# Shift of the first modulation by dot products on VectorE, its late columns behind the first emptying of PSUM, and the late modulation columns on GpSimd and ScalarE during attention

## The chip, the cores and the metric

The kernel runs on one core of one Trainium2 chip. The metric is the device time of one execution in microseconds (us). Five engines work from queues of their own, each in order: TensorE (PE, with its weight loads PEld), VectorE (DVE), ScalarE (ACT), GpSimd (POOL) and SyncE (SP), which issues most DMAs. Matrix products land in PSUM, everything else lies in SBUF.

## The reference: what is computed

One layer of an encoder with two head groups, over 1024 tokens of width 1024, all float32:

```python
mod = silu(c) @ w_ada + b_ada                 # 6 x 1024 columns
sh1, sc1, g1, sh2, sc2, g2 = split(mod, 6)
h = rms_norm(x, g) * (1 + sc1) + sh1
proj = h @ w_in                               # q, k, v | conv q/k, v, o, gates
y = concat(attention(q, k, v), bidirectional_mlstm(...))
x = x + g1 * (y @ w_out)
h = rms_norm(x, g') * (1 + sc2) + sh2
x = x + g2 * ((silu(h @ w_gate) * (h @ w_up)) @ w_down)
return rms_norm(x, g'')
```

Attention has 8 query heads on 2 key heads, with a norm and a rotary turn on q and k. The mLSTM has 4 heads, run forward and backward in chunks, behind a convolution over 5 tokens. The 48 groups of 128 modulation columns are 48 dot products of `silu(c)` with rows of the transposed `w_ada`.

## The kernel before: stages, queues and names

The kernel is written with an explicit order. A small event clock inside it (`Clock`, `Engine`, `Stream`) estimates the engines while the program is built, and the instructions are emitted in the order in which that clock reaches them. So an edit at one place moves instructions at others, far behind it. Nothing is moved when the program runs: each engine executes its list as written, and waits where an operand isn't there. Every matrix product of two float32 operands is done as three products of rounded parts (`mm3`, lines 307 to 310): `whi*x_hi`, `whi*x_lo`, `wlo*x_hi`; `whi` is made by ACT, `wlo` by POOL or DVE.

The stages, with their place in the profiled execution:

- **Opening, 0 to about 198 us.** The first three products (k, v and the first q pair; tiles `acc`, 6 PSUM banks) are computed from `x * sc1` without the root of the norm and without the shift. The norm's root is applied when PSUM is emptied (`vt`, `raw_q`: the DVE rows `vt<-acc` and `raw_q<-acc`), and the shift's part, a number per output column, is added later: `shift_sums` (line 621) multiplies the three weight blocks, loaded a second time as `wagain`, with the shift column `sh2` in 24 small matmuls (line 629). Its result `shift` releases `shifted` in `v_steps` and `rope_steps`. The other products need the complete `h` (tiles `hh`, `hl`, made by `h_steps`, line 664: DVE multiply, ACT affine with shift column `mod[:, k]`, ACT rounding, POOL remainder). `chunk_step` fills `acct` tiles from `h`, which take the PSUM banks of the first products as these come free. After that come the gates of the mLSTM (`gate_steps`: scans on DVE, transposes `T` on PE, results `cols` and `dec`) and the first units of `IN`, until `rope_ok[3]` and `gates_ok` are there.
- **Attention, about 198 to 512 us.** Three streams, `scores` (tile `S`, softmax on DVE, ACT, POOL: `sst`, `P`), `turned` (transposes `T` into `PT`) and `values` (`av`), 64 blocks. Where none of them can go on, PE is given units of `IN`, the remaining input projections: `f` (convolution, tile `acc`, `xp`, `y`) and `t` (tile `acct`).
- **mLSTM, 512 to about 690 us.** Streams of states (`U`, `Cs`), fronts (`E`, `W`) and backs (`na`, `ni`, `num`); the rest of `IN` and then the output projection (`o`) fill the gaps.
- **FFN, to the end.** It fills PE almost wholly.

The modulation columns: 16 large tiles `ada` (128x1024) in the opening give scale and shift; columns 4 to 7 of the shift wait for the flag `late` besides, which is set with the norm's root (line 707). The other 32 groups come as 64 half tiles (128x512) through `ada_late` (line 1069): at most two in flight, each one DMA on SP and one DVE multiply with `accum_out`. It is called from the opening's loops, from `ready()`, once in each of the 64 blocks of `scores`, and with each step of the streams in the mLSTM. 48 of them must be done at the end of attention; the last 16 follow in the mLSTM, and when `IN` has run out there, a loop (`while not summed`) emits what is left of the 16 before anything else.

Of the kernel before, what the change touches and what calls it, by code (L numbers as in the profile page):

```python
# [247 lines left out]
def layer_kernel(ctx, tc, xT, c, w_ada, vecs, cons, rope, w_f, w_t0, w_t, w_o, w_gu, w_d, out):  # L248
# [112 lines left out]
    with tc.manual_schedule():  # L361
# [161 lines left out]
        sh2 = stp.tile([P, KT, 2], F32, name="sh2")  # L523
# [97 lines left out]
        def shift_sums():  # L621

            ck.need(slot("acc").flag())
            acc, f = psum_tile([P, 3, 2], "acc")
            for f3 in range(3):
                ck.need(again[f3])
                w = wagain[f3].rearrange("p (a b) -> p a b", a=KT)
                for k in range(KT):
                    nc.tensor.matmul(acc[:, f3], w[:, k], sh2[:, k], start=k == 0, stop=k == KT - 1)
# [10 lines left out]
            ck.chain(LAT, take, gains, flag=shift_ok)  # L640
# [37 lines left out]
        for k in range(KT):  # L678
# [15 lines left out]
            if k == 5:  # L694
# [12 lines left out]
                ck.chain(0.0, *rstd_ok, lambda: None, flag=late)  # L707
# [1560 lines left out]
```

## Time and profile before

| | |
|---|---|
| runs | 1410.9 us median of 3 (1406.38 to 1412.68) |
| profiled execution | 1413.44 us, of it span 1411.7 us |
| PE busy | 1291.5 us (91%), mean granted clock 0.958 |
| DVE, ACT, POOL busy | 1068.9 us (76%), 673.2 us (48%), 634.4 us (45%) |
| half tiles `ada` on DVE, 52.4 to 197.7 us, 197.7 to 512 us, 512 to 690 us | 36.61 us (with 4 of the large), 16.65 us, 14.23 us |

Rows of a timeline give start, length, engine, line, operation, `out<-in`, shapes, and in brackets how long the engine had stood idle and who released it. L96 is the helper that records every operation of DVE, ACT and POOL, so these are told apart by their tiles. A windows row gives the busy time of each engine in that stretch, then the granted clock of PE, the DMA share and GB/s. A row of grouped instructions gives busy time and mean ns of one.

### The profile page before, as it was taken

Reading aid. Unit: us, or ns where it says so; the run is one execution under the profiler, and the core shown is the slowest. Engines: PE = TensorE matmul, PEld = TensorE weight load, DVE = VectorE, ACT = ScalarE, POOL = GpSimd, SP = SyncE. Lnnn points to the kernel's source line nnn. Section 1 sums busy time; section 2 is a strip of 40 time slices with the busy share of each in tenths; the row PEclk is TensorE's granted clock in tenths of the full one; section 3 lists DMA queues with packets and bytes.
Section 4 is the critical chain, followed back from the end, with each engine's and each line's share of the span. In section 5 each row is a group of like instructions: output and inputs, shape, how many; then the busy total and the mean of one; then the engine's idle time right before and its main releaser. Section 6 shows DMA issues by size and latency. Waiting matters only on the chain.

```text
span 1411.7 us, 19611 instructions
## 1 busy us (share of the span) xinstructions
PE 1291.5 (91%) x6632; PEld 1087.6 (77%) x6640; DVE 1068.9 (76%) x1623; ACT 673.2 (48%) x1217; POOL 634.4 (45%) x537
## 2 busy tenths in 40 slices
PE   7799779999999993989799799999999999979997
PEld 5597658898888892877677588888888887857887
DVE  7948989977888634888598897666766654998876
ACT  6654336576666652555377423233323333444462
POOL 0445434344444224667403165455455445545542
PEclk9889879999999996999899899999999999989999
DMA  9554542322122146633454243233222248733324
GB/s 353 179 165 146 161 157 72 113 72 56 54 70 60 51 141 205 226 115 117 140 168 145 70 152 102 105 113 112 103 82 94 96 164 310 303 84 102 98 64 154
DMA packets 103892, 185.98 MB, mean 132 GB/s; under 512 B 11376, under 2 KB 33136, under 8 KB 103792
## 3 DMA queue, kind: packets, MB, share of 16 engines
q1 hardware_dynamic: 90400, 162.63, 36.1%
q10 hardware_dynamic: 13392, 22.10, 4.1%
q8 instruction: 53, 0.87, 0.3%
q14 instruction: 47, 0.39, 0.1%
HBM read 137.76 MB, written 43.25 MB: 128 GB/s over the span
## 4 chain that ended last, share of the span: by engine, by line
PE 63%; DVE 22%; issue 5%; DMA 4%; ACT 3%; POOL 2%; SPq 0%; ACTq 0%; DVEq 0%; POOLq 0%
PE acc L310 16%; PE acc L309 16%; PE acc L308 16%; PE av L1164 3%; DVE sst L96 3%; DVE ada L96 3%; DVE y L96 3%; PE T L1145 2%; PE S L1113 2%; DVE PT L96 2%; DVE x L96 2%; PE acct L308 2%; PE acct L309 1%; PE acct L310 1%; DMA ada<-in_w_ada_dram 1%
## 5 line engine op out<-in xcount | busy, mean ns | idle before, releaser
L96 POOL TENSOR_TENSOR wlo<-wst,whi 128x512 fp32r<-128x512 f32 (+2 forms) x187 | 264.3, 1420 | 297.3 <-ACT whi L96 266.7
L96 ACT ACTIVATE whi<-wst 128x512 fp32r<-128x512 f32 (+2 forms) x219 | 130.9, 605 | 106.2 <-PE acc L310 32.9
L96 POOL TENSOR_SCALAR P<-P,sst 128x1024 f32<-128x1024 f32 x64 | 81.8, 1279 | 163.8 <-DVE sst L96 136.8
L309 PE MATMUL acc<-x,whi 128*128 128x512 f32 x352 | 138.4, 393 | 5.9 <-DVE x L96 5.9
L96 POOL TENSOR_TENSOR wlo<-wr,whi 128x512 fp32r<-128x512 f32 x56 | 77.7, 1388 | 75.2 <-ACT whi L96 70.5
L308 PE MATMUL acc<-whi,wch 128*128 128x512 f32 x244 | 96.5, 396 | 7.0 <-ACT wch L96 7.0
L310 PE MATMUL acc<-whi,wcl 128*128 128x512 f32 x244 | 96.7, 396 | 2.9 <-DVE wcl L96 2.8
L308 PE MATMUL acc<-hh,whi 128*128 128x512 f32 x224 | 96.2, 429 | 2.2 <-ACT xp L96 2.1
L96 DVE SCALAR_TENSOR_TENSOR ada<-ada,cond 128x512 f32<-128x512 f32 (+1 forms) x80 | 81.4, 1029 | 21.4 <-DMA ada<-in_w_ada_dram 13.0
L309 PE MATMUL acc<-wlo,wch 128*128 128x512 f32 x244 | 96.1, 394 | 0.1
L96 DVE TENSOR_TENSOR PT<-T,PT 128x512 fp32r<-128x512 f32 x128 | 83.5, 683 | 13.8 <-ACT PT L96 13.4
L96 ACT ACTIVATE P<-S,sst,colq 128x1024 f32<-128x1024 f32 x64 | 77.2, 1207 | 33.7 <-DVE sst L96 32.5
L96 ACT ACTIVATE PT<-T 128x512 fp32r<-128x512 f32 x128 | 72.1, 596 | 38.1 <-PE T L1145 37.4
L309 PE MATMUL acc<-hl,whi 128*128 128x512 f32 x224 | 90.0, 402 | 0.0
L308 PE MATMUL acct<-whi,hh 128*128 128x256 f32 (+1 forms) x256 | 80.0, 312 | 11.0 <-DVE vt L96 9.9
L310 PE MATMUL acc<-hh,wlo 128*128 128x512 f32 x224 | 89.9, 402 | 0.0
L96 ACT ACTIVATE whi<-wr 128x512 fp32r<-128x512 f32 x60 | 37.9, 632 | 105.1 <-DVE wr L96 50.1
L96 DVE TENSOR_TENSOR sg<-acc,sg 128x512 f32<-128x512 f32 x67 | 45.4, 687 | 55.7 <-PE acc L310 55.5
L96 POOL TENSOR_TENSOR wlo<-s,whi 128x512 fp32r<-128x512 f32 x40 | 53.9, 1349 | 67.2 <-ACT whi L96 67.2
L96 DVE TENSOR_REDUCE sst<-S 128x1 f32<-128x1024 f32 x64 | 77.8, 1216 | 6.8 <-PE S L1113 6.5
L309 PEld LDWEIGHTS acc<-x,whi 128*128 128x128 f32 x352 | 66.7, 189 | 21.0 <-DVE x L96 7.3
L96 DVE TENSOR_TENSOR wcl<-wd,wch 128x512 fp32r<-128x512 f32 x50 | 50.7, 1028 | 37.6 <-ACT wch L96 27.1
(474 smaller groups left out, 3812.1 us busy)
## 6 DMA issues: line engine op xcount, KB each, us to landing
wr<-in_w_gu_dram SPq DMA_DIRECT2D x66, 256.0 KB, 2.7
ada<-in_w_ada_dram SPq DMA_DIRECT2D x64, 256.0 KB, 3.2
wd<-in_w_d_dram SPq DMA_DIRECT2D x22, 512.0 KB, 7.0
wst<-in_w_gu_dram SPq DMA_DIRECT2D x34, 256.0 KB, 3.0
wst<-act_d SPq DMA_DIRECT2D x33, 256.0 KB, 4.8
ada<-in_w_ada_dram SPq DMA_DIRECT2D x16, 512.0 KB, 6.8
wst<-in_w_o_dram SPq DMA_DIRECT2D x32, 256.0 KB, 3.5
act_d<-sg ACTq DMA_DIRECT2D x31, 256.0 KB, 2.2
```

The lines of the kernel that those rows point to most:

```text
L96: return fn(*args, **kw)
L308: nc.tensor.matmul(acc, w[0], x[0], start=first, stop=False)
L309: nc.tensor.matmul(acc, w[0], x[1], start=False, stop=False)
L310: nc.tensor.matmul(acc, w[1], x[0], start=False, stop=last)
L1113: nc.tensor.matmul(sp[:, halves(n)], qs[:, j * P:(j + 1) * P], k2[g][m][:, halves(n)], start=m == 0, stop=m == 1)
L1145: nc.tensor.transpose(tp[:, k], Pt[q][:, (4 * b + k) * P:(4 * b + k + 1) * P], ident)
L1164: nc.tensor.matmul(av, va[:, k, h // 4], PT[it][m][:, k], start=(k, m) == (0, 0), stop=(k, m) == (NJ - 1, 1))
```

## The change

1. **Shift's part.** ACT writes a `diag` tile: 8 blocks of the identity, each scaled by one shift column. PE multiplies it by `ones` in two 128x512 matmuls, which leaves the shift as a row in every partition, in two PSUM banks of the `acc` ring. DVE multiplies it with the transposed weights (`w_fT`, a new input of the same bytes as the three blocks of `w_f`) in six 128x512 operations with `accum_out`, and adds the halves. The 24 small matmuls go.
2. **Late columns.** `late` is now set when the six first PSUM banks are empty, so the four large DVE products of shift columns 4 to 7 stand behind `vt` and `raw_q`. The remainder `hl` of the first tile is made by DVE, not POOL. The PSUM bank of the second half of query 1 is taken after the chunk loop.
3. **Modulation columns.** `ada_late` isn't called in the opening any more. The first 48 half tiles all fall to attention, and there each is a POOL multiply and an ACT copy with `accum_out`. The last 16 stay on DVE in the mLSTM.

```diff
@@ shift_sums
-                for k in range(KT):
-                    nc.tensor.matmul(acc[:, f3], w[:, k], sh2[:, k], start=k == 0, stop=k == KT - 1)
...
+                rows.append(psum_tile([P, HALF], "acc"))
+                nc.tensor.matmul(rows[i][0], ones, diag[0][:, halves(i)], start=True, stop=True)
...
+                dve.scalar_tensor_tensor(w, w, 1.0, rows[i][0], op0=OP.mult, op1=OP.mult, accum_out=sh2[:, f3, i:i + 1])
...
+                dve.tensor_add(shift, sh2[:, :, 0], sh2[:, :, 1])
...
+                act.activation(diag[0][:, k * P:(k + 1) * P], ident, AF.Copy, scale=mod[:, k:k + 1])
@@ load_again
-                again[i] = ck.chain(dma(w, w_f[i].rearrange("p a b -> p (a b)")), lambda: None)
+                again[i] = ck.chain(dma(w, w_fT[i]), lambda: None)
@@ h_steps
-                lambda: gps.tensor_sub(h_lo[k][:, halves(n)], xs, h_hi[k][:, halves(n)].bitcast(F32)))
+                lambda: (gps if n or k else dve).tensor_sub(h_lo[k][:, halves(n)], xs, h_hi[k][:, halves(n)].bitcast(F32)))
@@ the opening's order
-                ck.chain(0.0, *rstd_ok, lambda: None, flag=late)
+        ck.chain(0.0, *[f for a in acc0 for _, f in a], lambda: None, flag=late)
...
-                ada_late()
@@ ada_late
+            if n < 48:
+                adas.append(ck.chain(dma(t, w_ada[j][:, halves(i)]), lambda: gps.tensor_mul(t, t, PP["cond"][:, halves(i)]),
+                                     lambda: act.activation(t, t, AF.Copy, accum_out=modacc[:, i, j:j + 1]),
+                                     bg=["gps", "act"]))
+                return
@@ ready
-            if ck.t > t_ada[0]:
-                ada_late()
-                t_ada[0] = ck.t + 1.0
```

How it moves the engines' lists, at three places. First DVE behind the norm's root in the opening, where the first PSUM banks are emptied (`vt`, `raw_q`); `x` rows are the multiplies of `h_steps`:

```order
-L96 SCALAR_TENSOR_TENSOR ada,modacc<-ada,cond 128x1024 x4
 L96 TENSOR_TENSOR vt<-acc,sq 128x512
+L96 TENSOR_TENSOR raw_q_259<-acc,sq 128x512
+L96 TENSOR_TENSOR raw_q_257<-acc,sq 128x512
+L96 TENSOR_TENSOR vt<-acc,sq 128x512
+L96 TENSOR_TENSOR hl_230<-x_248,hh_222 128x512
 L96 TENSOR_TENSOR raw_q_259<-acc,sq 128x512
 L96 TENSOR_TENSOR raw_q_257<-acc,sq 128x512
 L96 TENSOR_TENSOR x_251<-x_251,ms 128x512
 L96 TENSOR_TENSOR x_252<-x_252,ms 128x512
+L96 SCALAR_TENSOR_TENSOR ada,modacc<-ada,cond 128x1024 x4
```

The four large products have gone from ahead of the six PSUM reads to behind them and two of the `x` rows, with one `hl` row between.

Second DVE in the mLSTM, from the first half tiles there; before:

```order
L96 SCALAR_TENSOR_TENSOR ada,modacc<-ada,cond 128x512 x2
L96 SCALAR_TENSOR_TENSOR Cs<-Cs,dec,U 128x130 x2
L96 SCALAR_TENSOR_TENSOR W<-tr,W 128x256 x2
L96 SCALAR_TENSOR_TENSOR ada,modacc<-ada,cond 128x512 x2
L96 SCALAR_TENSOR_TENSOR Cs<-Cs,dec,U 128x130 x2
L96 SCALAR_TENSOR_TENSOR W<-tr,W 128x256 x2
L96 SCALAR_TENSOR_TENSOR ada,modacc<-ada,cond 128x512 x12
L96 TENSOR_TENSOR mod<-modacc,vec 128x8
```

The same stretch of DVE's list now:

```order
L96 SCALAR_TENSOR_TENSOR ada,modacc<-ada,cond 128x512 x2
L96 SCALAR_TENSOR_TENSOR Cs<-Cs,dec,U 128x130 x2
L96 SCALAR_TENSOR_TENSOR ada,modacc<-ada,cond 128x512
L96 SCALAR_TENSOR_TENSOR W<-tr,W 128x256 x2
L96 SCALAR_TENSOR_TENSOR ada,modacc<-ada,cond 128x512
L96 SCALAR_TENSOR_TENSOR W<-tr,W 128x256 x2
L96 SCALAR_TENSOR_TENSOR ada,modacc<-ada,cond 128x512
L96 SCALAR_TENSOR_TENSOR Cs<-Cs,dec,U 128x130 x2
L96 SCALAR_TENSOR_TENSOR ada,modacc<-ada,cond 128x512
```

The run of twelve is broken up; the last of the 16 stands behind the first head's states, fronts and backs and among the second head's states. PE's list moved with it: between the last `av` and the first mLSTM transpose stood 87 matmuls of the projections, now 36, and in all 84 of these matmuls (128x256) have gone from attention to the mLSTM, where they now run on to the end of the second head's fronts. 12 matmuls 128x512 have gone from the opening to attention.

Third POOL in the middle of attention, after the change (before, this list has only the `P`, `wlo` and `qs` rows; `P` is the softmax's scaling):

```order
L96 TENSOR_SCALAR P<-P,sst 128x1024
L96 TENSOR_TENSOR ada<-ada,cond 128x512
L96 TENSOR_SCALAR P<-P,sst 128x1024
L96 TENSOR_TENSOR qs<-qd,qs 64x1024
L96 MEMSET xp 128x2 x2
L96 TENSOR_TENSOR wlo<-wst,whi 128x512
L96 TENSOR_SCALAR P<-P,sst 128x1024
L96 TENSOR_TENSOR ada<-ada,cond 128x512 x2
L96 TENSOR_SCALAR P<-P,sst 128x1024 x2
L96 TENSOR_TENSOR ada<-ada,cond 128x512
```

The 48 multiplies are spread from just ahead of the first `qs` to five blocks before the last.

More of the change, by code (lines that the diff above doesn't have):

```diff
@@ L247, in layer_kernel @@
 @with_exitstack
-def layer_kernel(ctx, tc, xT, c, w_ada, vecs, cons, rope, w_f, w_t0, w_t, w_o, w_gu, w_d, out):
+def layer_kernel(ctx, tc, xT, c, w_ada, vecs, cons, rope, w_f, w_fT, w_t0, w_t, w_o, w_gu, w_d, out):
     nc = tc.nc
@@ L522, in layer_kernel @@
         b1 = stp.tile([P, KT], F32, name="b1")
-        sh2 = stp.tile([P, KT, 2], F32, name="sh2")
+        sh2 = stp.tile([P, 3, 2], F32, name="sh2")
         shift = stp.tile([P, 3], F32, name="shift")
@@ L621, in shift_sums, with dot @@
         def shift_sums():
[L623 to L627, printed above, removed]
-                for k in range(KT):
-                    nc.tensor.matmul(acc[:, f3], w[:, k], sh2[:, k], start=k == 0, stop=k == KT - 1)
-                    ck.pe(0.23)
+            ck.need(diag_ok)
+            rows = []
+            for i in range(2):
+                ck.need(slot("acc").flag())
+                rows.append(psum_tile([P, HALF], "acc"))
+                nc.tensor.matmul(rows[i][0], ones, diag[0][:, halves(i)], start=True, stop=True)
+                ck.pe(0.86)
+            def dot(f3, i):
+                w = wagain[f3][:, halves(i)]
+                dve.scalar_tensor_tensor(w, w, 1.0, rows[i][0], op0=OP.mult, op1=OP.mult, accum_out=sh2[:, f3, i:i + 1])
+                if f3 == 2:
+                    rows[i][1].set(ck, ck.fin + LAT)
             def take():
-                dve.tensor_copy(shift, acc[:, :, 0])
-                f.set(ck, ck.fin + LAT)
+                dve.tensor_add(shift, sh2[:, :, 0], sh2[:, :, 1])
             def gains():
@@ L638, in gains, with diagonal @@
                     act.activation(shiftg[:, f3:f3 + 1], shift[:, f3:f3 + 1], AF.Copy, scale=V(n))
-            ck.chain(LAT, take, gains, flag=shift_ok)
+            dots = [ck.chain(LAT, again[f3], lambda f3=f3: [dot(f3, i) for i in range(2)]) for f3 in range(3)]
+            ck.chain(LAT, *dots, take, gains, flag=shift_ok)
+        diag, diag_ok = [], Flag()
+        def diagonal():
+            diag.append(bp.tile([P, S], F32, tag="big", name="diag"))
+            for k in range(KT):
+                act.activation(diag[0][:, k * P:(k + 1) * P], ident, AF.Copy, scale=mod[:, k:k + 1])
+        ck.chain(0.0, *sh_ok, diagonal, flag=diag_ok)
         wagain, again = {}, {}
@@ L2052, in layer_kernel @@
             load_piece()
-        ck.chain(0.0, *sh_ok, lambda: act.activation(sh2, mod[:, 0:KT, None].to_broadcast([P, KT, 2]), AF.Copy), load_again)
+        ck.chain(0.0, *sh_ok, load_again)
         ck.chain(0.0, y_free, load_tables)
@@ L2059, in layer_kernel @@
                 tiles.append(psum_tile([P, 272], "acct"))
-            ck.need(slot("acc").flag())
-            accs.append(psum_tile([P, HALF], "acc"))
+            if n == 0:
+                ck.need(slot("acc").flag())
+                accs.append(psum_tile([P, HALF], "acc"))
             def chunk_step(k):
@@ L2090, in layer_kernel @@
                 ck.chain(0.0, *vo_ok[0], gate_steps)
+                ck.need(slot("acc").flag())
+                accs.append(psum_tile([P, HALF], "acc"))
                 for k in range(KT):
@@ L2240, in layout @@
     tk = lambda a: a.reshape(8, P, -1).transpose(1, 0, 2)
+    o["w_fT"] = c_(o["w_f"][0:3].transpose(0, 3, 2, 1).reshape(3, P, 1024))
     o["w_t0"] = c_(tk(np.concatenate([gt, w_in[:, 1792:2048]], 1)))
```

4 lines of the change are left out of this document (1 added, 3 removed).

## The prediction

> **What bounds the kernel now.** I read the windows by stage first, then the waits of PE in each, then the timelines at the longest waits. The windows (start:end, length, then busy us of PE, PEld, DVE, ACT, POOL, granted clock, DMA) for opening, attention, mLSTM and the rest:
>
> ```profile
> 52.40:197.70 145.30, 119.24 (x607) 102.98 (x607) 117.02 (x176) 68.11 (x105) 77.64 (x50) 0.85 0.50 152
> 197.70:512.00 314.30, 300.68 (x1991) 269.76 (x1992) 255.44 (x431) 198.42 (x352) 128.36 (x101) 0.98 0.23 70
> 512.00:690.00 178.00, 137.54 (x766) 116.45 (x774) 120.37 (x271) 79.57 (x207) 103.89 (x145) 0.90 0.51 163
> 690.00:1411.00 721.00, 688.96 (x3104) 566.13 (x3102) 533.78 (x667) 293.94 (x499) 324.32 (x238) 0.98 0.40 133
> ```
>
> PE is the bound: it idles 26.1 us of 145.3 in the opening, 13.6 of 314.3 in attention, 40.5 of 178.0 in the mLSTM. Its work is the same in sum wherever the units stand, so a stage is worth what it loses in idle time and in clock. The rest after 690 us has the same lists before and after. PE's waits in the opening, in attention, and one in the mLSTM:
>
> ```profile
> PE acct L308 <- DVE vt L96: 9.9, 2, 8.8
> PE T L1033 <- DVE cols L96: 6.8, 1, 6.8
> PE T L947 <- DVE gI L96: 3.5, 1, 3.5
> PE ms L763 <- ACT sqk L96: 3.2, 2, 2.0
> ...
> PE T L1145 <- DVE PT L96: 6.8, 12, 2.5
> PE S L1113 <- ACT P L96: 3.8, 1, 3.8
> ...
> PE T L1145 <- POOL P L96: 0.7, 1, 0.7
> ...
> PE ni L1949 <- DVE num L96: 8.2, 9, 2.1
> ```
>
> Every long one names DVE. The longest of all is in PE's timeline of the mLSTM, with DVE's half tiles inside those 21.4 us (window row, DVE busy and count with the accumulator reads), the last of them, and the DMA queue there:
>
> ```profile
> 559.24 2.07 PE L1865 MATMUL U<-wv,kt 128*128 128x260 f32 x4 [21.44 <-DVE Cs L96]
> ...
> 537.80:559.20 21.40, 8.54 (x22) 0.55 0.64 184
> ...
> 557.85 0.69 DVE L96 SCALAR_TENSOR_TENSOR ada<-ada,cond 128x512 f32<-128x512 f32 x1 [1.58 <-DMA ada<-in_w_ada_dram]
> ...
> 539.62 15.29 SPq L313 DMA_DIRECT2D ada<-in_w_ada_dram x9
> ```
>
> Eleven half tiles run here one behind the other, each waiting for its load, two in flight, and `Cs` stands behind them on DVE, `U` behind `Cs` on PE.
>
> **The change, part by part. 1: shift's part.** PE's timeline in the opening:
>
> ```profile
> 51.73 0.39 PE L309 MATMUL acc<-hl,whi 128*128 128x512 f32 x1
> 51.96 0.39 PE L310 MATMUL acc<-hh,wlo 128*128 128x512 f32 x1
> 61.14 0.57 PE L308 MATMUL acct<-whi,hh 128*128 128x272 f32 x1 [8.80 <-DVE vt L96]
> ...
> 65.48 0.63 PE L308 MATMUL acc<-hh,whi 128*128 128x512 f32 x1
> 65.91 0.63 PE L309 MATMUL acc<-hl,whi 128*128 128x512 f32 x1
> ...
> 69.27 0.39 PE L308 MATMUL acc<-hh,whi 128*128 128x512 f32 x1
> ...
> 83.19 7.62 PE L629 MATMUL acc<-sh,wagain 128*128 128x2 f32 x48
> 90.67 0.57 PE L308 MATMUL acct<-whi,hh 128*128 128x272 f32 x1
> ```
>
> The small matmuls hold PE 7.5 us (83.2 to 90.7). Two 128x512 matmuls of float32 take their place; two such with `ones` are the next row, with the price of four 128x128 ACT scalings and that of a DVE product with one operand in PSUM:
>
> ```profile
> 42.30 1.88 PE L698 MATMUL ms<-ssx,ones 128*128 128x512 f32 x4
> ...
> 527.59 1.14 ACT L96 ACTIVATE W<-E,cols 128x128 f32<-128x128 f32 x4
> ...
> 60.32 0.68 DVE L96 TENSOR_TENSOR vt<-acc,sq 128x512 f32<-128x512 f32 x1
> ```
>
> So PE gains 7.5 - 1.9 = 5.6 us. `diag` costs ACT 8/4 x 1.14 = 2.3 us, ahead of `hh` of blocks 5 to 7 (below). The six dot products have one operand in PSUM, as `vt` has, so 6 x 0.68 = 4.1 us. They start when the rows are there, near 82 us, so `shift` comes near 87 us instead of behind 90.7, beside PE's second chunk loop, which needs none of it. The second row takes a bank that `vstg` empties, about 1 us of waiting: net 4.6. The wait also brings PE to half rate: after the 8.8 us gap, matmuls of 512 columns come 0.43 us apart against 0.23 before it, until 69; 7.9 us at half rate lose 3.9. For the 128x2 stretch, after which PE also comes back at 0.57 a matmul, I take 2.8.
>
> **2: late columns.** DVE and POOL there:
>
> ```profile
> 52.53 1.22 DVE L96 SCALAR_TENSOR_TENSOR ada<-ada,cond 128x1024 f32<-128x1024 f32 x1
> ...
> 53.67 2.31 DVE L96 SCALAR_TENSOR_TENSOR ada<-ada,cond 128x1024 f32<-128x1024 f32 x1
> ...
> 53.62 5.68 POOL L96 TENSOR_TENSOR hl<-x,hh 128x512 fp32r<-128x512 f32 x3 [53.20 <-ACT hh L96]
> ```
>
> `vt` can begin at 52.5, when PE is done, not 60.3. Six reads at 0.6 and `hl` end near 57; PE starts for good near 56.2, when `hl` of the first tile is there, and loses about 4 us instead of 9.9. But the four products now run from 58.5 to 67 (2.3 each while POOL runs beside them, 1.2 without, by the two rows), then two shift columns, `diag` 2.3 and three affines on ACT: `hl` of block 5 is ready near 73.7, where PE arrives at 71.5. New wait 2.1. Net gain 3.8, and 2 of clock.
>
> **3: no half tiles in the opening, POOL and ACT in attention.** Grouped rows, opening first, then attention:
>
> ```profile
> L96 DVE SCALAR_TENSOR_TENSOR ada<-ada,cond 128x512 f32<-128x512 f32 (+1 forms) x33 | 36.4, 1120 | 0.0
> ...
> L96 POOL TENSOR_SCALAR P<-P,sst 128x1024 f32<-128x1024 f32 x64 | 81.8, 1279 | 163.8 <-DVE sst L96 136.8 <-PE av L1164 19.0 <-PE T L1145 4.0
> L96 ACT ACTIVATE PT<-T 128x512 fp32r<-128x512 f32 x124 | 69.8, 596 | 37.2 <-PE T L1145 36.4
> L96 POOL TENSOR_TENSOR wlo<-wst,whi 128x512 fp32r<-128x512 f32 x20 | 28.4, 1424 | 14.1 <-ACT whi L96 12.6 <-DVE sst L96 1.3
> L96 DVE SCALAR_TENSOR_TENSOR ada<-ada,cond 128x512 f32<-128x512 f32 x19 | 16.5, 868 | 0.3 <-DMA ada<-in_w_ada_dram 0.2
> L96 ACT ACTIVATION_READ_ACCUMULATOR P<-S,sst,colq 128x1 f32 x64 | 12.4, 194 | 0.0
> ```
>
> 29 of the 33 go from the opening, some 28 us of DVE in a stretch where it is busy 117 of 145. The chain of `gate_steps` runs on DVE, so the waits for `gI`, `cols` and `sqk` (13.5 us) shrink. Not to nothing: shorter covers bring PE to `gI` about 5 us early, and 3 and 2 us stay at the others. Gain 3.5, with 3 of clock. The first `ada` multiply stands ahead of the first `qs` on POOL: 1.4 lost. The 12 matmuls that leave the opening (2.7 us) come back in attention. Opening in sum: 4.6 + 2.8 + 3.8 + 2 + 3.5 + 3 - 1.4 = 18.3 us.
>
> In attention POOL gets 48 x 1.42 = 68 us on top of 128 of 314, ACT 48 x (0.60 + 0.19) = 38 on 198; DVE loses 16.5. Queued behind a multiply is `P`, and PE's transposes wait for `P`; behind the ACT copy stand the exponentials and `PT`. The cover is POOL's own idle time: 163.8 us ahead of the 64 `P`, 2.6 us each, and a multiply of 1.42 fits into that. Where the cover is gone, each one costs its 1.42. The bounds: a gain up to the 6.8 us of waits for `PT` with DVE freed, or a loss up to 10, half the multiplies showing 0.4. I take 0, as `T <- POOL P` is only 0.7 now. The loads (256 KB each) move to a stage whose DMA share is 0.23.
>
> **4: the hole of the mLSTM.** The loop that emits the rest of the last 16 ran because only 132 matmuls of `IN` were left to cover the loads. Now 216 are left, and DVE's list shows no run of half tiles: the 21.4 us and the cold start go. Against it, the end of attention and the second transposes:
>
> ```profile
> 509.77 2.08 PE L1164 MATMUL av<-PT,va 128*128 128x256 f32 x16
> ...
> 524.15 0.41 PE L1837 MATMUL tr<-ident,mk 128*128 128x128 f32 x2 [1.14 <-issue]
> ...
> 560.00:570.00 10.00, 10.00 (x47) 8.44 (x47) 5.74 (x17) 2.96 (x10) 3.19 (x8) 0.80 0.78 262
> ```
>
> The cold start is (1 - 0.80) x 10 = 2 us. PE reached the transposes 12.3 us after the last `av`, behind 87 matmuls (0.13 each, as the `av` row's); with 36 it arrives 6.6 us earlier at the same load: 6.6 lost. Net 21.4 + 2 - 6.6 = 16.8.
>
> **Sum.** 18.3 + 0 + 16.8 = 35.1 us, from 1413.4 (span 1411.7 and 1.7 around it) to 1378.3. The profiled execution lies 2.5 us over the median of the runs, 1410.9; there it is 1376.
>
> **Two rules weighed.** The rows show half rate for 7.9 us after a gap. The Trainium skill, "TensorE: Matmul & The Clock Gate", Part 1, says that an idle window of about 3.4 us throttles and a busy one of the same length releases; as an estimate a gap would then lose 1.7 us, not 3.9, and my 7.8 us of clock in the opening would be about 4: 1380. For part 3, GpSimd takes 1.42 us where DVE takes 0.87 by the rows, and DVE's large products doubled from 1.22 to 2.31 beside POOL. "GPSIMD Engine Reference" of the Trainium skill, Engine selection, says to keep elementwise multiplies on VectorE, and Specifications says that the SBUF interface is shared with DVE instructions of two SBUF inputs: the trace agrees on both, and the first rival is what this would make.
>
> **The rivals.**
> - *Slower: POOL's queue sets attention's pace.* Every multiply shows: 48 x 1.42 = 68 us against a gain of 35, so 1411 + 33 = 1444. It breaks even at 0.73 us shown per multiply. For: POOL's list alternates `ada` and `P` to the end, and ACT waits for POOL in order. Against: POOL would be busy 196 of 314, and the gaps of 2.6. Chance 0.07.
> - *The hole only moves:* the longer cover of `IN` meets mLSTM waits that are there anyway (`num`, 8.2), and PE idles elsewhere. Then the opening alone: 1411 - 18 = 1393. Chance 0.17.
> - *The opening gives nothing:* late blocks 5 to 7, the row banks and `gI` eat it. Then 1411 - 17 = 1394. Chance 0.11.
> - *The change does nothing measurable,* both at once or the lists shift other waits in: about 1408. Chance 0.06.
> - *Attention speeds up too:* DVE's 16.5 us off and shorter gate waits than I hold: 1360. Chance 0.12.
>
> **How the numbers follow.** My forecast has 0.47: 1376, alone 1366 to 1387. A measurement of this kernel can tell about 0.5% (7 us) from no change. Faster: 0.47 + 0.17 + 0.11 + 0.12 = 0.87; same 0.06; slower 0.07. The range 1356 to 1399 takes in the forecast with attention's bounds (-6.8, +10), the two one-sided cases, and most of the fast one.
>
> **What would show it.** Right: the first `S` near 177 us instead of 198; `acct` behind `vt` waits under 5 us; no PE wait over 8 us between 500 and 600; granted clock of the opening over 0.88; attention's PE idle under 16 us. Wrong: `T <- POOL P` or `T <- ACT PT` above 15 us in attention, a wait at `U` or `tr` of 15 us, or PE idling 26 us in the opening again.

## The result: a third of the forecast gain, and the profile after

| | before | changed |
|---|---|---|
| runs, median of 5 | 1407.8 us (1406.1 to 1412.7) | 1396.7 us (1394.3 to 1397.8) |
| span of the profiled execution, granted clock | 1411.7 us, 0.958 | 1396.0 us, 0.972 |

The ratio is 0.991 (95% interval 0.989 to 0.994): 0.9% faster, where 2.5% was forecast. The time lies inside the range, near the prices of the rivals "the hole only moves" (1393) and "the opening gives nothing" (1394). The profiled execution of before (1413.4) lies 5.7 us over the median of its runs, that of the changed kernel (1397.8) 1.1 us, so differences of spans are about 4.6 us larger than those of medians.

The windows of the changed kernel by stage, cut at the first `S`, the end of the last `av` and the last transposes of `hs` (columns as in the prediction):

```profile
52.40:191.28 138.88, 109.81 (x551) 92.48 (x551) 96.83 (x132) 68.63 (x112) 76.98 (x49) 0.88 0.37 108
191.28:505.67 314.39, 293.39 (x1917) 258.85 (x1915) 248.42 (x392) 225.38 (x439) 189.65 (x145) 0.99 0.29 88
505.67:672.46 166.79, 146.65 (x853) 124.63 (x852) 117.22 (x271) 81.86 (x212) 109.33 (x147) 0.97 0.56 181
672.46:1396.00 723.54, 690.71 (x3112) 566.49 (x3111) 533.97 (x668) 295.36 (x501) 325.66 (x240) 0.98 0.40 133
```

DVE has 20 us less in the opening, as meant, and POOL 61 us more in attention. PE's idle time is 138.88 - 109.81 = 29.1 us in the opening (before 26.1), 21.0 in attention (13.6) and 20.1 in the mLSTM (40.5). PE's waits in those three stages:

```profile
PE T L1046 <- ACT T L96: 7.5, 1, 7.5
PE T L960 <- DVE gI L96: 7.1, 1, 7.1
PE T L1046 <- DVE cols L96: 4.8, 1, 4.8
PE acct L308 <- ACT hh L96: 3.0, 2, 1.9
PE acct L310 <- DVE hl L96: 2.6, 1, 2.6
...
PE T L1163 <- DVE PT L96: 14.4, 13, 2.9
PE S L1131 <- ACT P L96: 1.9, 1, 1.9
...
PE ni L1967 <- DVE num L96: 6.1, 7, 1.9
PE tr L1855 <- issue: 4.3, 1, 4.3
```

The hole of 21.4 us at `U` is gone, and so is the wait of 9.9 behind `vt`, at whose place 2.6 for `hl` is left. In their place stand 19.4 us at the gates' transposes (`T`; before 11.4 with `ACT T` 1.1) and 14.4 at `PT` (before 6.8).

**Stage by stage, with moved work taken off.** A stage's length alone misleads, since projection matmuls move between the stages. So for each kernel I take the length of a stage, less that of before, and subtract what the moved matmuls last: 0.227 us for one of 512 columns and 0.12 for one of 256, their distances in PE's timeline. In before the first `S` starts at 197.70, the last `av` ends at 511.85, the last transposes of `hs` start at 687.49. For the changed kernel: the opening 191.28 - 197.70 = -6.4, with 12 matmuls of 512 fewer (2.7), so -3.7; attention 314.4 - 314.2 = +0.2, with 12 of 512 more and 84 of 256 fewer (7.4 less in sum), so +7.6; the mLSTM 166.8 - 175.6 = -8.9, with those 84 (10.1) in addition, so -18.9. The rest is -0.7. Forecast were -18.3, 0 and -16.8. The table gives all kernels by the same rule. Its ratios are of medians, but the three other columns come from one execution of each kernel, which lies up to 6 us from its median: parts 1 and 2 were profiled 3.9 us below it, the change with its half tiles on DVE 6.2 below, the row "attention later" 5.9 above. Where a kernel has the lists of before in a stage, the stage agrees within about 1 us (-0.3, -0.4, +1.1).

| kernel | ratio to before (95%) | opening | attention | mLSTM |
|---|---|---|---|---|
| the change (parts 1, 2, 3) | 0.991 (0.989 to 0.994) | -3.7 | +7.6 | -18.9 |
| part 1 alone | 0.998 (0.997 to 0.999) | -3.7 | +1.9 | -4.3 |
| part 2 alone | 0.995 (0.993 to 0.997) | -6.5 | -0.4 | +1.1 |
| part 3 alone | 0.988 (0.986 to 0.990) | -5.0 | +5.2 | -19.2 |
| parts 1 and 2 | 1.005 (1.003 to 1.007) | +6.7 | -0.8 | -5.8 |
| parts 1 and 3 | 0.982 (0.981 to 0.984) | -10.2 | -0.7 | -20.3 |
| parts 2 and 3 | 0.979 (0.977 to 0.980) | -9.9 | -1.8 | -19.8 |
| before, up to 64 half tiles in attention | 0.990 (0.988 to 0.991) | -0.3 | -0.2 | -17.4 |
| the change, v tiles staged apart | 0.988 (0.986 to 0.991) | -8.2 | +6.9 | -19.0 |
| the change, staged apart and `gI` early | 0.984 (0.981 to 0.986) | -11.6 | +9.3 | -20.1 |
| parts 1 and 2, v tiles staged apart | 0.999 (0.998 to 1.001) | +1.5 | -0.8 | -6.1 |
| parts 2 and 3, staged apart and `gI` early | 0.986 (0.984 to 0.989) | -11.6 | +7.4 | -21.4 |
| the change, half tiles of attention on DVE | 0.991 (0.989 to 0.993) | -5.9 | +3.8 | -18.7 |
| parts 2 and 3, half tiles of attention on DVE | 0.986 (0.984 to 0.988) | -10.6 | +9.2 | -20.1 |
| the change, multiplies on POOL twice | 1.006 (1.004 to 1.008) | -4.2 | +32.8 | -20.8 |
| the change with gate edits, attention later | 0.997 (0.996 to 0.999) | -5.5 | +4.9 | -2.9 |
| parts 2 and 3, up to 64 half tiles in attention | 0.972 (0.971 to 0.974) | -9.5 | -2.0 | -29.2 |

### The profile page after: what moved, and what is told of

Same layout as the page of the kernel before. It is cut to its first block, busy times and chain, and to the rows that moved or that the text cites. A ratio compares the mean times of both kernels' runs of the same rounds, so it can differ in the third digit from the quotient of the medians.

```text
span 1396.0 us, 19590 instructions
## 1 busy us (share of the span) xinstructions
PE 1285.8 (92%) x6596; PEld 1074.8 (77%) x6596; DVE 1038.7 (74%) x1540; ACT 704.3 (50%) x1320; POOL 701.8 (50%) x584
## 4 chain that ended last, share of the span: by engine, by line
PE 61%; DVE 16%; issue 9%; ACT 5%; DMA 4%; POOL 3%; SPq 1%; DVEq 0%; ACTq 0%; POOLq 0%
PE acc L309 15%; PE acc L310 15%; PE acc L308 15%; PE av L1182 3%; PE T L1163 3%; DVE y L96 3%; PE S L1131 2%; DVE x L96 2%; DVE sst L96 2%; DVE PT L96 2%; POOL wlo L96 1%; PE acct L310 1%; PE acct L308 1%; PE acct L309 1%; DVE Cs L96 1%
## 5 line engine op out<-in xcount | busy, mean ns | idle before, releaser
L96 POOL TENSOR_TENSOR wlo<-wst,whi 128x512 fp32r<-128x512 f32 (+2 forms) x187 | 262.2, 1408 | 260.2 <-ACT whi L96 230.0
L96 POOL TENSOR_TENSOR wlo<-wr,whi 128x512 fp32r<-128x512 f32 x56 | 78.2, 1397 | 75.6 <-ACT whi L96 70.9
L1163 PE MATMUL T<-ident,P 128*128 128x128 f32 x512 | 70.9, 276 | 14.6 <-DVE PT L96 14.4
L96 ACT ACTIVATE PT<-T 128x512 fp32r<-128x512 f32 x128 | 71.7, 596 | 20.5 <-PE T L1163 19.8
L96 POOL TENSOR_TENSOR ada<-ada,cond 128x512 f32<-128x512 f32 x48 | 71.6, 1494 | 18.5 <-DMA ada<-in_w_ada_dram 18.4
```

The costliest lines, as they stand in the source:

```text
L96: return fn(*args, **kw)
L1163: nc.tensor.transpose(tp[:, k], Pt[q][:, (4 * b + k) * P:(4 * b + k + 1) * P], ident)
```

## The experiments

**The parts one by one.** Each of the three kernels is before with one part of the diff. Part 1 alone (dot products), part 2 alone (`late` and the first `hl`), part 3 alone (`ada_late` out of the opening, the `n < 48` branch). Their cores, one behind the other:

```diff
@@ part 1
-                    nc.tensor.matmul(acc[:, f3], w[:, k], sh2[:, k], start=k == 0, stop=k == KT - 1)
+                dve.scalar_tensor_tensor(w, w, 1.0, rows[i][0], op0=OP.mult, op1=OP.mult, accum_out=sh2[:, f3, i:i + 1])
@@ part 2
-                ck.chain(0.0, *rstd_ok, lambda: None, flag=late)
+        ck.chain(0.0, *[f for a in acc0 for _, f in a], lambda: None, flag=late)
@@ part 3
-                ada_late()
+            if n < 48:
+                adas.append(ck.chain(dma(t, w_ada[j][:, halves(i)]), lambda: gps.tensor_mul(t, t, PP["cond"][:, halves(i)]),
```

> The kernel before with part 1 alone: shift's part by two 128x512 matmuls and six dot products. Half tiles stay where they were (33 in the opening, on DVE), but in the mLSTM DVE's list now shows a last run of 6 half tiles instead of 12. Theory A (the opening keeps what PE's shorter work gives, and no more; the hole of the mLSTM is worth about 11 us net when it goes wholly): first S about 4 to 5 us earlier with the cover counted in, the wait at U behind Cs about halved, time 1408 - 4 - 5 = 1399. As the forecast had it (4.6 + 2.8 in the opening, and half of 16.8): 1408 - 7 - 8 = 1393. Rival (the opening gives back all that part 1 saves, as longer waits at gI and cols): 1408 - 5 = 1403, and the waits of PE for gI, cols and sqk in sum 5 us longer than the 13.5 of before.

> The kernel before with part 2 alone: the four late products behind the emptying of PSUM, first hl on DVE. The lists of attention and of the mLSTM hold the same matmuls as before, so any difference is the opening's. Forecast: acct waits behind vt under 5 us instead of 9.9, and 3.8 + 2 us less in all: 1402. Theory A (the gates' chain of DVE, ACT and POOL sets the end of the opening, and PE that comes earlier only waits longer there): the wait at vt shrinks as forecast, the waits at gI and cols grow by nearly as much, time 1406 to 1408.

> The kernel before with part 3 alone: no half tile in the opening, 48 on POOL and ACT in attention, 16 on DVE in the mLSTM, there in runs of at most two but for the first. Forecast: opening -5 (waits for gI, cols and sqk shrink from 13.5 to about 10, clock 3, first qs 1.4 later), attention 0, mLSTM -17, in all 1408 - 22 = 1386. Theory A (DVE's load by half tiles did not set the gate chain): waits for gI, cols and sqk stay within 2 us of 13.5, mLSTM -11, time 1397. Rival C (POOL and ACT in attention cost what the opening wins): first S 5 us earlier for the same matmuls, but waits for P and PT in attention up by 5 us or more, time 1397 as well; the waits by stage tell A and C apart.

All three are faster: 1406.0, 1403.1 and 1391.7 us against 1409.9 of before beside them. Part 2 came as forecast (1402), part 3 between its forecast and the rivals (1386 and 1397), and part 1 slower than all three of its expectations (1393 to 1403). Their terms in the opening are -3.7, -6.5 and -5.0, in sum -15.2 against the forecast 18.3. Theory A, that the opening gives back what comes earlier, does not hold for parts 2 and 3: with part 2 the wait at `vt` goes, and `gI` and `cols` stay at 4.3 and 5.4; part 3 alone keeps 10.7 us of waits for gates and query norms (forecast about 10). Its attention lost 5.2 us, so rival C has something too. Part 1 alone gives back half, as theory A has it: its two longest waits at the gates are

```profile
PE T L961 <- DVE gI L96: 8.1, 1, 8.1
PE T L1047 <- ACT T L96: 3.6, 1, 3.6
```

and with `whi` (2.8) and `dexp` (0.7) PE waits 15.2 us there, where before it waited 11.4. Most of what the forecast missed appears only where parts meet.

**The hole by itself.** Before, with one line of `scores` changed:

```diff
-                ada_late()
+                ada_late(64)
```

> The kernel before with one edit: the blocks of scores may call up to 64 half tiles instead of 48, so that none is left for the mLSTM and the hole there can't form; opening's list as before; DVE has 16 more half tiles in attention, and 96 matmuls of the projections go from attention to the mLSTM. It prices the hole by itself. If the hole was worth what the forecast says (21.4 + 2 - 6.6): 1408 - 17 = 1391. If PE in the mLSTM then meets other waits as in the changed kernel (net 11): 1397. If the hole only moves: 1408, with PE waits over 8 us at na, ni, tr or U.

1395.4 us against 1409.9, between the two expectations (1391 and 1397); the mLSTM gives 17.4, and its waits keep `num` at 7.7 and `tr` at 3.9. The medians differ by 14.5 us in all, so the forecast's size (16.8) was right within 2 or 3 us, without any of the three parts.

**The parts in pairs.** The same diffs, two at a time:

> Parts 2 and 3 together, without the dot products. By stage, with the projection matmuls moved between the stages taken off, the parts alone gave in the opening -3.7 (part 1), -6.5 (part 2) and -5.0 us (part 3), in sum -15.2, and the whole change -3.7. If they add (no interaction of these two): opening -11.5, attention +5 (as part 3 alone), mLSTM -19, together 1410 - 25 = 1385. If one limit lies under both (the gates' chain behind the norm's root, on DVE, ACT, POOL and SP in order, which PE reaches earlier and waits for): opening -5 to -6.5, time 1391, and PE's waits for gI, T and cols longer than part 3 alone has (8.8 us in sum).

> Parts 1 and 3 together, without the late columns. The lists hold the same number of projection matmuls in every stage as with parts 2 and 3. If they add: opening -8.7, attention +5, mLSTM -19: 1410 - 23 = 1387. If one limit lies under both: opening -4 to -5, time 1391 to 1392. If the dot products are what spoils the sum (their two PSUM banks and their six DVE operations stand ahead of the gates on DVE): opening near 0, time 1396, and the wait at gI over 7 us here but not with parts 2 and 3.

> Parts 1 and 2 together, half tiles where they were. So far, by stage and with moved matmuls taken off: parts 2 and 3 together -9.9 in the opening, parts 1 and 3 -10.2, all three -3.7. If it is the pair of parts 1 and 2 that spoils it (both bring PE earlier to the first chunk's end, so that the four copies of v tiles on ACT are listed ahead of the key norm's root, where the last one stops for a store): the opening here gains 4 us or less instead of 10, the wait at gI is 7 us or more, time 1408 - 4 - 4 (half tiles' run in the mLSTM half as long) = 1400. If only all three together do that: opening -10, time 1394.

Parts 2 and 3 add up and more: 1377.7 us, where the sum was 1385. Parts 1 and 3 also: 1383.4. But parts 1 and 2 together take 1415.6 against 1408.6 of before: slower, though each alone is faster, and slower than either expectation (1400 and 1394). The opening loses 6.7 us there, where the two parts alone give 10.2 in sum. In the changed kernel all three stand together, and its opening keeps 3.7.

Where that comes from shows on ACT. First parts 2 and 3, ACT's timeline behind the first chunk loops:

```profile
94.77 0.69 ACT L96 ACTIVATE sq<-ms,both 128x512 f32<-128x512 f32 x1 [3.67 <-PE ms L755]
...
106.80 0.94 ACT L96 ACTIVATE vstg<-acct 128x256 f32<-128x256 f32 x3 [2.93 <-DVE gs L96]
109.20 0.38 ACT L96 ACTIVATE vstg<-acct 128x256 f32<-128x256 f32 x1 [1.47 <-DMA v_d<-vstg]
```

The root of the key norm (`sq<-ms`) stands ahead of the four copies `vstg` of the second chunk loop, as in before. Now parts 1 and 2:

```profile
97.21 0.93 ACT L96 ACTIVATE vstg<-acct 128x256 f32<-128x256 f32 x3
105.62 0.38 ACT L96 ACTIVATE vstg<-acct 128x256 f32<-128x256 f32 x1 [7.49 <-DMA v_d<-vstg]
105.90 0.68 ACT L96 ACTIVATE sq<-ms,both 128x512 f32<-128x512 f32 x1
```

and the changed kernel, its lines of ACT, SP, DVE and PE in turn:

```profile
99.06 0.94 ACT L96 ACTIVATE vstg<-acct 128x256 f32<-128x256 f32 x3 [0.43 <-DVE gs L96]
104.16 0.38 ACT L96 ACTIVATE vstg<-acct 128x256 f32<-128x256 f32 x1 [4.17 <-DMA v_d<-vstg]
104.44 0.68 ACT L96 ACTIVATE sq<-ms,both 128x512 f32<-128x512 f32 x1
...
97.57 2.41 SPq L313 DMA_DIRECT2D sw<-raw_q  x4
...
100.70 4.19 SPq L313 DMA_DIRECT2D v_d<-vstg  x4
...
105.16 0.69 DVE L96 TENSOR_SCALAR sq<-ms 128x512 f32<-128x512 f32 x1 [5.89 <-ACT sq L96]
...
110.45 2.28 DVE L96 TENSOR_TENSOR raw_q<-raw_q,sw 128x1024 f32<-128x1024 f32 x1
...
113.80 0.28 DVE L96 COPY gI<-gs 128x64 f32<-128x64 f32 x2
...
114.23 1.09 PE L960 MATMUL T<-ident,gI 128*128 128x128 f32 x4 [7.12 <-DVE gI L96]
```

With parts 1 and 2 together PE is early enough that the builder lists the four `vstg` ahead of the key norm's root. They have three buffers. So the fourth waits until the first is stored, that store stands on SP behind eight DMAs `sw<-raw_q` (four of them shown), and the root, DVE's rotary turn behind it and the gates' `gI` behind that all wait with ACT. PE stands at the gates' first transposes for 7.1 us (9.4 with parts 1 and 2).

**Taking that stop away.** The lists stay as they are; the last four v tiles get one 128x1024 tile of the `x` ring, which is free by then, in place of the `vstg` ring:

```diff
-            stg = bp.tile([P, 2, P], F32, tag="vstg", name="vstg", bufs=3)
+            if ci == 0 and j >= 4:
+                if j == 4:
+                    vx.append(stp.tile([P, 4, 2, P], F32, tag="x", name="vx", bufs=KT))
+                stg = vx[0][:, j - 4]
+            else:
+                stg = bp.tile([P, 2, P], F32, tag="vstg", name="vstg", bufs=3)
```

In the changed kernel, and in parts 1 and 2:

> The changed kernel with the first of the two edits alone: the last four v tiles are staged in one tile of their own. All lists are those of the changed kernel. ACT's stop of 4.2 us for the store goes. If that stop is what delays the gates: the gI copies come 4 us earlier, the wait at gI is about 3, first S 4 us earlier, time 1397 - 4 = 1393. If the stop is covered (DVE's rotary turn ends no earlier): the wait at gI stays at 7 and the time at 1397; then the place of the gI copies is worth the whole of the two edits.

> Parts 1 and 2 together (1.0049 of before, slower), with the last four v tiles staged in one tile of their own, as in the run that gave the changed kernel 5 us; lists as without it. In parts 1 and 2 together ACT stopped 7.5 us for the store, ahead of the key norm's root. If that stop makes the pair slower: the gI copies come 7 us earlier, the wait at gI goes from 9.4 to 4 or less, time 1415 - 7 = 1408. If the later waits (whi, dexp, T: 16 us) take it over: first S within 2 us of 205.8, time 1414.

The changed kernel goes to 1391.5 us, 5 less (expected 4), its opening from -3.7 to -8.2; its wait at `gI` falls from 7.1 to 4.9 (expected about 3). Parts 1 and 2 go from 1415.6 to 1408.0 (expected 1408), the opening from +6.7 to +1.5. There the wait at `gI` stayed at 6.1, more than I expected, as DVE's turn runs on to 111.9 in front of `gI`. So the stop is shown to cost 4.5 us of the opening in the changed kernel and 5.2 in the pair. That is a third of what the pair loses against the sum of its parts (from -10.2 to +6.7, 16.9 us). The rest of that loss was not taken apart: with the stop gone the pair's PE still waits 8.4 us for `whi`, 6.1 for `gI` and 4.9 for `dexp`.

The second edit puts `gI` behind the query norm's means instead of behind the turn:

```diff
+                def place():
+                    for d in range(2):
+                        dve.tensor_copy(gI[0][:, :, :, 32 * d:32 * d + 4],
+                                        gs[:, :, 8 * d:8 * d + 8].rearrange("p j (t x) -> p j t x", t=2))
...
-                ck.chain(0.0, *vo_ok[0], gate_steps)
+                ck.chain(0.0, *ev_ok, place, gate_steps)
```

`ev_ok` is set when PSUM is emptied, not when the tile is stored, and `rows(0)` loses its copies. Both edits in the changed kernel, and in parts 2 and 3:

> The changed kernel with two edits in the gates' chain: the last four v tiles of the first chunk loop are staged in one tile of their own, so that ACT's list doesn't stop 4.2 us for the store of an earlier one; and the two gI copies stand on DVE right behind the means of the query norm instead of behind seven operations of the rotary turn. PE's list is the same. The wait at gI (7.1 us) should go to under 1. If the lost lead was made there: first S 5 to 7 us earlier, time 1391. If the chain behind it is the limit (softplus on ACT, scans and cols on DVE, in order with the rotary turn): PE waits for T and cols that much longer, first S within 2 us of 191.3, time 1396.

> Parts 2 and 3 (1378) with the two edits of the gates' chain that gave 9.5 us to the changed kernel. Opening: the wait at gI is 4.1 and the ACT stop for a store 1.5, so 3 to 4 us are to be had. But the lists of attention and of the mLSTM now hold the same matmuls as the changed kernel's (276 of 512 columns and 360 of 256 in attention, seven convolution units there instead of six). Theory L (the loss of attention belongs to that list: more of the convolution's taps on DVE beside POOL's multiplies): attention loses 7 to 9 us as in the changed kernel, PE's waits for PT 13 to 15, time 1383. Theory D (the loss in attention comes with the dot products of part 1): attention -2 as with parts 2 and 3, time 1374.

In the changed kernel, DVE and PE:

```profile
101.24 0.29 DVE L96 COPY gI<-gs 128x64 f32<-128x64 f32 x2
...
104.66 0.60 PE L966 MATMUL T<-ident,gI 128*128 128x128 f32 x4
```

No wait is left there, the first `S` comes at 183.4 instead of 191.3, and the time is 1387.2 (0.984; 1391 expected): the opening now gives 11.6. Behind it the waits for `T` (7.5) and `cols` (4.5) are as long as ever, so the lead went through the chain, and the rival that these would swallow it falls. With parts 2 and 3 the same edits make the kernel slower, 1388.1 instead of 1377.7 (theory L expected 1383): the opening gains 1.7, the mLSTM 1.6, and attention loses 9.2 (the profiled executions are 5 us apart, the medians 10). Theory D, that attention's loss comes with the dot products, falls: there are none in it.

**Attention.** Half tiles back on DVE, in the changed kernel and in parts 2 and 3; and the multiply done twice:

```diff
@@ on DVE
-            if n < 48:
...
@@ twice
-                adas.append(ck.chain(dma(t, w_ada[j][:, halves(i)]), lambda: gps.tensor_mul(t, t, PP["cond"][:, halves(i)]),
+                adas.append(ck.chain(dma(t, w_ada[j][:, halves(i)]), lambda: (gps.tensor_mul(t, t, PP["cond"][:, halves(i)]), nc.gpsimd.tensor_mul(t, t, PP["cond"][:, halves(i)])),
```

> The changed kernel with its 48 half tiles of attention on DVE, as one multiply with accumulation each, instead of POOL and ACT. The changed kernel lost 7.6 us in attention once the moved matmuls are taken off (part 3 alone 5.2). If that is POOL's and ACT's extra work (DVE's own operations slower beside POOL, PT behind the copies on ACT): attention's loss goes to 2 us or less, PE's waits for PT there from 14.4 to about 7, time 1397 - 6 = 1391. If DVE is what PT waits for anyway, 48 x 0.87 = 42 us more on DVE make it worse: waits for PT 20 us or more, time 1402. If neither: 1397.

> Parts 2 and 3 (1378), but with the 48 half tiles of attention on DVE as one multiply each. Attention's matmuls differ by 3 from that version. If GpSimd's and ACT's share of the half tiles cost nothing there (attention -1.8 with them): DVE has 42 us more, PT waits grow from 5.8 to 8 or more, time 1380 to 1383. If they do cost and the list hid it: 1374.

> The changed kernel with each of the 48 multiplies on GpSimd done twice, the second one not known to the builder's clock, so that all lists are the same but for the added instructions (the modulation columns come out wrong). The dose is 48 x 1.42 = 68 us more on POOL in attention. If the loss of 7.6 us there comes from POOL's multiplies (DVE's taps slower beside them, 1.81 us against 1.44, so PT late): taps go to 2 us or more and attention loses about as much again, time 1404 or more. If it comes from the list and ACT alone: attention within 2 us of 314.4, time 1397. If POOL's queue then sets attention's pace (P late): waits for P over 15 us, time above 1415.

In the changed kernel DVE instead of POOL takes 1395.8 us, no difference that can be told from 1396.7. In parts 2 and 3 it costs 11.5 us (1389.2), against both my guesses: attention goes from -1.8 to +9.2. The second multiply, whose columns are then no longer those of the layer, adds 20 us (1417.1); attention loses 25.2 more for 66 us more of POOL. PE waits for `P` of POOL only 3.3 us there and for `PT` 17.0, so neither of the two mechanisms expected for this run explains it: its PE idles 37.4 us instead of 21.0, and its granted clock is 0.97 instead of 0.99. The steps of the convolution on DVE, grouped rows in attention, of before:

```profile
L96 DVE SCALAR_TENSOR_TENSOR y<-xp,vec,y 128x1024 f32<-128x1024 f32 x28 | 40.2, 1437 | 0.5
```

of the changed kernel, beside POOL's multiplies:

```profile
L96 DVE SCALAR_TENSOR_TENSOR y<-xp,vec,y 128x1024 f32<-128x1024 f32 x28 | 50.8, 1813 | 0.4
...
L96 POOL TENSOR_TENSOR ada<-ada,cond 128x512 f32<-128x512 f32 x47 | 69.6, 1484 | 16.8 <-DMA ada<-in_w_ada_dram 16.8
```

of parts 2 and 3, and with the multiply done twice:

```profile
L96 DVE SCALAR_TENSOR_TENSOR y<-xp,vec,y 128x1024 f32<-128x1024 f32 x24 | 40.9, 1705 | 0.2
```

```profile
L96 DVE SCALAR_TENSOR_TENSOR y<-xp,vec,y 128x1024 f32<-128x1024 f32 x27 | 50.6, 1873 | 0.3
...
L1095 POOL TENSOR_TENSOR ada<-ada,cond 128x512 f32<-128x512 f32 x47 | 66.1, 1407 | 3.7
```

These steps, the taps, are slower by a quarter in the changed kernel. But twice the dose hardly slows them more, and with parts 2 and 3 the same 48 multiplies cost attention nothing. One by one, a tap beside no POOL instruction takes 1.27 to 1.29 us in all four kernels; 15 of 28 are such in before, 4 of 28 in the changed kernel, 2 of 24 with parts 2 and 3 and none with the multiply done twice. So there were hardly any left to be slowed.

With one and the same matmul counts in attention (276 of 512 columns, 360 of 256) the loss is 7.6, 6.9, 9.3 and 7.4 us in four kernels, with and without dot products; with another list (243 and 384) it is -1.8, -0.7 and -2.0 in three. So with the same multiplies on POOL the loss goes with the list. That is a correlation; no run shows which place in the list makes it. Attention with parts 2 and 3, to be compared with its row of the changed kernel:

```profile
192.55:492.94 300.39, 285.94 (x1907) 254.00 (x1907) 241.78 (x387) 223.28 (x438) 192.18 (x145) 1.00 0.31 94
```

PE idles 14.5 us here and 21.0 there, and the granted clock is 1.00 against 0.99, about 3 us of 314 by estimate: together the 9.4 us between the two. One try at giving the repaired kernel another list:

```diff
-            return rope_ok[3].done and gates_ok.done and not open_sum[0]
+            return rope_ok[3].done and gates_ok.done and len(convs) > 1 and convs[1].done and not open_sum[0]
```

> The changed kernel with both gate edits (1387), and attention may only start when the second convolution unit is stored: 75 matmuls of 512 columns go from attention to the opening, 51 of 256 from the mLSTM to attention, and 20 of the taps instead of 25 stand in attention. The work on GpSimd is the same. If attention's loss of 7 to 9 us belongs to the list (taps and PT beside the multiplies): 4 us of it or more go, time 1382. If it belongs to the 48 multiplies and copies whatever the list: attention +7 to +9 again, time 1387. The shorter cover of the mLSTM (165 matmuls of 256 instead of 216) may bring back part of the hole there: then 5 us more.

It took 1403.7 us, where 1382 to 1392 was expected. Attention's loss went from 9.3 to 4.9, as expected; with fewer taps in attention this is not the list's order alone. But the opening lost 6.1 of its gain, and a hole of 10.0 us came back in the mLSTM, where the cover is now shorter (165 instead of 216 matmuls of 256) and six half tiles again run one behind the other on DVE, most of them waiting for their loads, ahead of `num`:

```profile
PE ni L1973 <- DVE num L96: 20.2, 8, 10.0
```

**The best version.** Parts 2 and 3 with the one line of the hole's experiment:

> Parts 2 and 3 (1378), and all 64 half tiles in attention, the last 16 on DVE there instead of in the mLSTM. Lists of the opening are the same. The mLSTM loses 14 us of DVE work, which its waits at num, W and Cs (4.3, 0.5, 0) hardly show: gain of 2 to 3 at most; attention gains 14 us of DVE work: 0 to 2 lost. Time 1376 to 1379. If DVE is attention's limit beside POOL: 1384.

1370.9 us, 0.972 (0.971 to 0.974), the fastest of all and below both kernels. It is not what I expected of it: only one half tile went from the mLSTM to attention, and the mLSTM gains 9.4 us more (the medians are 6.8 us apart). Windows there, of parts 2 and 3:

```profile
523.00:533.00 10.00, 8.73 (x53) 8.26 (x54) 8.17 (x29) 4.10 (x13) 3.11 (x5) 0.83 0.50 138
533.00:543.00 10.00, 6.63 (x48) 5.82 (x46) 9.30 (x25) 5.51 (x14) 6.67 (x9) 0.97 0.81 236
543.00:553.00 10.00, 7.58 (x32) 6.39 (x33) 8.27 (x14) 4.77 (x12) 8.60 (x10) 0.69 0.62 189
```

and with that line:

```profile
523.00:533.00 10.00, 9.75 (x72) 9.29 (x73) 9.32 (x29) 5.26 (x16) 3.61 (x6) 1.00 0.68 200
533.00:543.00 10.00, 7.63 (x50) 6.47 (x49) 9.76 (x28) 6.46 (x19) 8.26 (x9) 1.00 0.79 249
543.00:553.00 10.00, 9.60 (x48) 7.46 (x46) 6.20 (x12) 4.69 (x12) 10.00 (x18) 1.00 0.87 272
```

Gone are the waits of 5.3 for `hs` (up to 545.2) and of 4.5 for `yah` (up to 650.0), and the clock is full in these 30 us, where it was 0.69 to 0.97. Why one half tile does that was not tried; the lists differ from there on.

## Why the prediction was wrong, point by point

- **The opening, 18.3 forecast, 3.7 measured: the step that failed.** It reads "Opening in sum: 4.6 + 2.8 + 3.8 + 2 + 3.5 + 3 - 1.4 = 18.3". As terms of a part by itself two of three were right (7.4, 5.8 and 5.1 forecast, 3.7, 6.5 and 5.0 measured; the first is half). What failed is that they add. The sum takes the gates to be ready when PE comes earlier, but `gI` comes only 3.2 us earlier (113.8 instead of 117.0) and PE 6.9. At the gates and query norms PE was to wait 3.5 us less, and it waits 6.2 more (20.8 instead of 14.6): 9.7 of the missing 14.6 us. Shown as a cause is the order on ACT: with parts 1 and 2 together the stop for a store comes ahead of the key norm's root (4.5 us), and `gI` stands behind the turn on DVE (3.4 more). With that stop away and `gI` early the opening gives 11.6. The prediction names no row of ACT's list behind the second chunk loop. What is missing even then, 6.7 us, is about the size of the clock's terms, the second thing that failed.
- **The waits for `gI`, `cols` and `sqk` were to shrink** because DVE has less to do. With part 3 alone they did (10.7, forecast about 10). In the changed kernel those for `gI`, `cols` and `T` grew from 11.4 to 19.4, though DVE had 20 us less; only `sqk` (3.2) went, with 1.4 for `rqv` in its place. There the chain of the gates is held by what stands ahead of it in order on ACT, SP and DVE, and less load on DVE does not help.
- **The clock in the opening, 2.8 + 2 + 3 = 7.8 us forecast, about 1 by estimate.** PE's half-rate stretches up to 100 us, two of before and two of the changed kernel:

```profile
55.30:69.00 13.70, 6.74 (x25) 0.50 0.47 145
86.10:96.30 10.20, 10.20 (x48) 0.50 0.37 110
...
55.80:62.60 6.80, 5.86 (x23) 0.50 0.00 0
72.90:79.70 6.80, 6.00 (x24) 0.50 0.00 0
```

  One long wait has become two shorter ones, and half rate follows both. The large matmuls (`mm3`) at half rate last 6.7 and 4.4 us before (the rest of the 10.2 are the small ones, which the 4.6 counts, and some transposes), and 5.9 and 6.0 changed; behind 100 us they last 10.7 and 7.9. Half of the difference, (21.8 - 19.8) / 2, is 1 us. With both edits at the gates they last 22.0 us in all, so nothing is won there. The granted clock of the whole opening rises more, from 0.85 to 0.88, because waits and small matmuls count in it too. Of the two rules weighed neither is settled: behind its first long wait PE works at half rate for 7.9 us before and 5.9 in the changed kernel, but for 3.4 with the v tiles staged apart.
- **What came as forecast in the opening.** The changed kernel's PE, and DVE's `hl` and `shift`:

```profile
56.74 0.59 PE L310 MATMUL acct<-whi,hl 128*128 128x272 f32 x1 [2.60 <-DVE hl L96]
...
72.35 0.40 PE L308 MATMUL acct<-whi,hh 128*128 128x272 f32 x1 [1.93 <-ACT hh L96]
73.70 0.60 PE L310 MATMUL acct<-whi,hl 128*128 128x272 f32 x1 [0.83 <-POOL hl L96]
...
82.88 1.97 PE L628 MATMUL acc<-diag,ones 128*128 128x512 f32 x4
84.29 0.69 PE L308 MATMUL acct<-whi,hh 128*128 128x272 f32 x1
...
54.93 1.75 DVE L96 TENSOR_TENSOR hl<-x,hh 128x512 fp32r<-128x512 f32 x1
...
88.54 0.15 DVE L96 TENSOR_TENSOR shift<-sh 128x3 f32<-128x3 f32 x1
```

  PE starts for good at 56.7 (forecast 56.2) and waits for block 5 until 73.7 (73.7). The two row matmuls take 1.97 (1.9), `shift` is there at 88.5 (87). At 84.3 PE was 6.4 us ahead of before; at the first `S` still 6.4, with 2.7 of that moved work: the 3.5 and 3 us of part 3 never came on top. (The terms 4.6, 3.8 and 2 give 10.4 at 84.3; the second half-rate stretch takes most of the difference.) Of the five signs for "right" two were there, short waits behind `vt` and none over 8 us between 500 and 600; of those for "wrong" one, PE idling 29.1 us in the opening.
- **Attention, 0 forecast, +7.6 measured,** inside the bounds (-6.8 to +10). The multiplies cost POOL 69.6 us (68 forecast) and POOL's `P` is not waited for, as argued. The price is paid at `PT` (14.4 us of waits instead of 6.8), whose last step is on DVE. That the slower taps there (1.81 us instead of 1.44) make it is not shown: with parts 2 and 3 they take 1.71, and the waits for `PT` are 5.8. The runs show that the price goes with the list, from -1.8 to +9.3 with the same work on POOL, and that DVE instead is no cure. Which place in the list makes the difference stays open.
- **The mLSTM, 16.8 forecast, 18.9 measured:** right, and shown alone (17.4, the medians 14.5) and by its partial return with a shorter cover.
- **The rivals.** The time came near that of "the opening gives nothing" by luck: the opening gave 3.7, and attention took 7.6. Of its mechanism, "late blocks 5 to 7, the row banks and `gI`", only `gI` was a large part; block 5 was waited for 2.8 us (2.1 forecast). The hole did not only move: the longest wait in the mLSTM is now 4.3 us. POOL's queue did not set attention's pace, and attention did not speed up.
- **The page on GpSimd.** The Trainium skill, "GPSIMD Engine Reference", Specifications, has the SBUF interface shared with DVE instructions of two SBUF inputs: the taps agree (1.44 to 1.81). Its advice in Engine selection, multiplies on VectorE, does not hold in every list: with parts 2 and 3 it costs 11.5 us.

## What to carry to other kernels

Don't add the gains of parts without looking at the lists of all together: here two pairs added up and the third did not. When two edits bring one engine earlier, compare the order of every engine that its next wait leads back to, ACT and the DMA queue too, and not only of the engine with the load. A copy into a ring of buffers that waits for a store holds up all that is listed behind it (4.2 and 7.5 us here), so look for such copies ahead of a chain. Measure the parts of a change one by one and in pairs: here all three parts gain 11 us, and two of them without the third 30.

## What the runs showed of the hardware that was not expected

DVE's taps beside POOL's multiplies take 1.81 us instead of 1.44, but with twice the multiplies only 1.87: the slowing does not grow in step with POOL's busy time, as 24 of the 28 already ran beside some POOL instruction. A POOL power of a 128x16 tile takes 2.9 to 4.9 us, where POOL scales a `P` of 128x1024 in 1.25; the changed kernel's rows:

```profile
125.56 2.90 POOL L96 TENSOR_TENSOR rqv<-rqv,both 128x16 f32<-128x16 f32 x1 [2.40 <-DVE rqv L96]
140.98 4.93 POOL L96 TENSOR_TENSOR rqv<-rqv,both 128x16 f32<-128x16 f32 x1 [2.43 <-DVE rqv L96]
...
L96 POOL TENSOR_SCALAR P<-P,sst 128x1024 f32<-128x1024 f32 x64 | 79.9, 1250 | 90.3 <-DVE sst L96 63.9 <-PE av L1182 16.0 <-PE T L1163 9.0
```
